# Down-projection of a gated MLP: seven half-size products in place of the plain product

## The chip, the core and the metric

One core of a Trainium2 chip runs the whole layer as one program. The metric is the device time of that program in microseconds (us); the time before, 3258.98 us, is the median of three runs (3258.03 to 3262.15). TensorE multiplies, VectorE and ScalarE work on SBUF and PSUM, GpSimd on SBUF alone, and SyncE's queue (SP) issues nearly all transfers between HBM and SBUF.

## The reference, cut to what matters

The layer has a token-mixing sublayer and a channel-mixing sublayer. Only the second one's end is touched. x is 2048 tokens x 1024, `w_up` 1024 x 5632, `w_down` 2816 x 1024, all float32.

```python
def conv_ffn(x, conv_w, conv_b, w_up, w_down):
    h = x @ w_up
    h = causal_depthwise_conv_width_3(h, conv_w) + conv_b
    gate, val = jnp.split(h, 2, axis=-1)
    return (jax.nn.silu(gate) * val) @ w_down

ffn = conv_ffn(x, ...)
x = layer_norm(ALPHA * x + ffn, ln2_g, ln2_b)      # the output, 2048 x 1024
```

## The kernel before

A float32 product is made of three passes: each operand is split into a high part (rounded to the multiplier's format, ScalarE) and a low part (the rest, VectorE), and `mm3` adds high x high, high x low and low x high into one PSUM bank. `split` and `split_new` make the parts.

The stages follow each other: projections, attention, `mix_out`, `ffn_up`, `ffn_down`. Each is a generator, and `run_to_end` calls `turn` after each step; `store` puts a transfer on a list that `turn` issues on SP one step later. Tiles come from pools: `T` is a slot of 4 KB a partition (42 of them), `M` one of 2 KB (8), `PS1` a PSUM bank (4), `PS2` a pair of banks (2 pairs). A new tile waits until the last user of its slot is done. The build orders each engine's instructions by when it reckons that they can start, so an engine's order is near the order of the program text but not the same.

`ffn_up` takes the tokens in two halves of 1024 (`hf`) and in each half the 22 column blocks (`NF`) of gate and value, already as seven half-size products (`product`, k = 0 to 6); in the second half the blocks run backwards and their split weights come back from HBM (`slot_back`, one block ahead). `after` adds the products from PSUM, `conv` does the convolution, the gate and the store of the block `h[hf][f]` (128 features x 1024 tokens) to HBM, spread over the next block's seven steps. After the last block the rest of `conv` runs by itself (line 1759).

`ffn_down` runs over `seq`: five parts of row blocks (4, 4, 4, 2 and 2 blocks of 128 tokens) x 22 feature blocks f. Each step loads one weight block of 128 x 1024 and the part's columns of one h block three steps ahead (`load`), splits them one step ahead (`split`), and issues 3 matmuls for each row block and column half: 24 a step in parts of four. The sums of a part stay in all 8 banks, or in 4. In the last step of a part VectorE adds ALPHA times the residual row (`load_rows`) to each bank, and `norm_stages` does the layer norm of each row block in stages, one a step: "A" takes the sums on ScalarE, "D" on VectorE; with "-" the gain and shift are VectorE's, otherwise the letters name the engines ("P" is GpSimd). The last two row blocks of all take "D".

Of the kernel before, what the change touches and what calls it, by code (L numbers as in the profile page):

```python
# [18 lines left out]
S, D = 2048, 1024  # L19
# [224 lines left out]

class Kern:
# [156 lines left out]
    def setup(self):  # L402
# [25 lines left out]
        self.d_h = [[self.DT([P, 2 * G], name="h") for _ in range(NF)] for _ in range(2)]  # L428
        self.I = {}
# [1210 lines left out]
    def ffn_up(self):  # L1640
# [6 lines left out]
        nc, cw = self.nc, self.cw  # L1647
        hl = self.C([P, 2 * NF, 2], name="hl")
# [43 lines left out]
        prep = Share(self.operands(1), 40, 7 * (NF - 2))  # L1692
        for i in range(2 * NF):
# [30 lines left out]
            for k in range(7):  # L1724
                ps = self.product(i, k)
                if i == NF - 1:
                    self.xo[k] = None
                    self.ffn_operand(1, k)
                if k:
                    after(k - 1, done)  # L1730
# [15 lines left out]
                if hf == 0 and f:  # L1746
                    prep.tick()
                    if i == NF - 2 and k == 6:
                        prep.flush()
                yield 2.7  # L1750
# [8 lines left out]
        for _ in work:  # L1759
            yield  # L1760

    def ffn_down(self):

        nc = self.nc
        parts = [(0, 4), (4, 4), (8, 4), (12, 2), (14, 2)]
        seq = [(n, f) for n in range(len(parts)) for f in range(NF)]
        raw, ready, rows = {}, {}, {}

        def load(j):
            if j >= len(seq):  # L1770
                return
            n, f = seq[j]
            b, m = parts[n]
            w, h = self.T([P, D]), self.M([P, m * P])
            nc.sync.dma_start(w, self.a["w_ffn_down"][0, f * P:(f + 1) * P, :])
            nc.sync.dma_start(h, self.d_h[b // 8][f][:, (b % 8) * P:(b % 8 + m) * P])
            raw[j] = w, h

        def split(j):
            if j >= len(seq):  # L1780
                return
            w, h = raw.pop(j)
            hp = self.T([P, 2, h.shape[1]], F32R)
            self.split(hp[:, 0], hp[:, 1], h)
            ready[j] = self.split_new(w), hp

        def load_rows(n):
            b, m = parts[n]
            rows[n] = []
            for i in range(b, b + m):  # L1790
                t = self.T([P, D])
                nc.sync.dma_start(t, self.d_x1[i // 8][i % 8])  # L1792
                rows[n].append(t)

        for j in range(3):
            load(j)
        split(0)
        gb = self.load_norm("ln2_g", "ln2_b")
        norming = []

        def norm_tick():
            for gen in list(norming):
                if next(gen, "end") == "end":
                    norming.remove(gen)

        for j, (n, f) in enumerate(seq):
            b, m = parts[n]
            if f == 0:
                if m == 4:
                    t = [self.PS2(), self.PS2()]  # L1810
                    banks = [t[i][:, c * 512:(c + 1) * 512] for i in range(2) for c in range(2)]
                    banks += [self.PS1() for _ in range(4)]
                elif n % 2:
                    banks = [self.PS1() for _ in range(4)]
                else:
                    t = [self.PS2(), self.PS2()]
                    banks = [t[i][:, c * 512:(c + 1) * 512] for i in range(2) for c in range(2)]
                load_rows(n)
            load(j + 3)
            split(j + 1)  # L1820
            (wh, wl), hp = ready.pop(j)
            for i in range(m):
                r = slice(i * P, (i + 1) * P)
                for c in range(2):
                    cs = slice(c * 512, (c + 1) * 512)
# [99 lines left out]
```

## Time and profile before

| | |
|---|---|
| time, median of 3 runs | 3258.98 us |
| profiled execution | 3255.52 us |
| its span, first to last instruction | 3253.7 us |
| TensorE busy | 3106.2 us, 95% |
| VectorE busy | 2415.8 us, 74% |
| ScalarE busy | 1613.8 us, 50% |
| GpSimd busy | 642.8 us, 20% |
| mean granted clock of TensorE | 0.984 of full speed |

Busy time is the sum of an engine's instruction durations over the span. The granted clock is the share of full speed that the chip gave TensorE. In the profile PE is TensorE, PEld its weight loads, DVE VectorE, ACT ScalarE, POOL GpSimd, SPq the transfer queue; tiles are named by pool: b is a `T` tile, m an `M` tile, p PSUM, xtmp and xraw scratch tiles. Line 133 is the helper through which all instructions are recorded, so rows are told apart by tiles and shapes.

### The profile page before, as it was taken

The numbers are of one execution on the slowest core, as the hardware profiler recorded it, in microseconds if no ns is written. First come the engines' busy times: TensorE is split into PE (matmuls) and PEld (weight loads), VectorE is DVE, ScalarE is ACT, GpSimd is POOL, SyncE is SP. The second block draws the span as 40 slices with busy tenths as digits, with TensorE's granted clock in tenths as the row PEclk, the third lists the DMA queues.
The fourth block names the chain that finished last, engine by engine and source line by source line (L and its number), as shares of the span: only waits on it lengthen the run. The fifth ranks groups of instructions, "written<-read, shape, count | busy, mean of one in ns | idle before, by whom it ended". The sixth has DMA issues, their size and how long they took to land. (4 is left out here: it accounts for less than half of the span.)

```text
span 3253.7 us, 44390 instructions
## 1 busy us (share of the span) xinstructions
PE 3106.2 (95%) x15014; PEld 2585.8 (79%) x15014; DVE 2415.8 (74%) x4642; ACT 1613.8 (50%) x3068; POOL 642.8 (20%) x592
## 2 busy tenths in 40 slices
PE   8998899999999999699999999999999999999998
PEld 8886688888888787488787877878788887888876
DVE  5589987987799989988766799889855555453465
ACT  3365746874678777577411244444432232442343
POOL 2027410010010211000412244445111111000000
PEclk9999899999999999899999999999999999999999
DMA  7667784754575332211546788788666665653554
GB/s 250 233 203 275 247 329 160 259 213 166 177 265 205 118 105 62 93 59 62 200 143 208 262 281 297 285 298 295 245 213 217 225 228 199 234 197 109 205 222 154
DMA packets 306833, 666.88 MB, mean 205 GB/s; under 512 B 25322, under 2 KB 130222, under 8 KB 306606
## 3 DMA queue, kind: packets, MB, share of 16 engines
q1 hardware_dynamic: 297966, 648.31, 56.6%
q10 hardware_dynamic: 8640, 15.73, 1.3%
q8 instruction: 119, 1.95, 0.2%
q14 instruction: 108, 0.88, 0.1%
HBM read 434.67 MB, written 229.28 MB: 204 GB/s over the span
## 5 line engine op out<-in xcount | busy, mean ns | idle before, releaser
L133 PE MATMUL p<-b,b 128*128 128x512 f32 (+3 forms) x12832 | 2888.3, 381 | 104.6 <-ACT b L133 37.9
L133 PEld LDWEIGHTS p<-b,b 128*128 128x128 f32 x12832 | 2305.6, 190 | 559.4 <-ACT b L133 40.7
L133 ACT ACTIVATE b<-p 128x512 fp32r<-128x512 f32 (+11 forms) x618 | 351.5, 603 | 245.8 <-PE p L133 235.5
L133 DVE TENSOR_TENSOR b<-p,b 128x512 fp32r<-128x512 f32 (+5 forms) x574 | 362.7, 652 | 148.5 <-PE p L133 102.7
L133 ACT ACTIVATE b<-b 128x1024 fp32r<-128x1024 f32 (+2 forms) x310 | 265.8, 874 | 305.3 <-DVE b L133 94.0
L133 ACT ACTIVATE m<-b,F 128x448 bf16<-128x448 f32 (+3 forms) x448 | 366.3, 821 | 87.9 <-DVE F L133 69.3
L133 DVE TENSOR_SCALAR_CACHE_REDUCE m<-b,F 128x512 bf16<-128x512 f32 (+6 forms) x476 | 370.0, 808 | 0.9
L133 DVE TENSOR_TENSOR b<-b,b 128x1024 fp32r<-128x1024 f32 (+4 forms) x224 | 282.9, 1268 | 72.4 <-ACT b L133 48.3
L133 POOL TENSOR_TENSOR b<-b,b 128x1024 f32<-128x1024 f32 (+3 forms) x94 | 231.5, 2464 | 480.5 <-DVE b L133 399.0
L133 DVE SCALAR_TENSOR_TENSOR b<-b,cw,b 128x1022 f32<-128x1022 f32 (+1 forms) x176 | 248.0, 1419 | 94.4 <-ACT b L133 93.5
L133 ACT ACTIVATE b<-m 128x512 fp32r<-128x512 f32 (+1 forms) x248 | 143.9, 587 | 301.0 <-DVE m L133 121.4
L133 ACT ACTIVATE b<-b,cw 128x1024 f32<-128x1024 f32 x88 | 106.8, 1236 | 290.0 <-DVE b L133 290.0
L133 DVE TENSOR_TENSOR b<-m,b 128x512 fp32r<-128x512 f32 (+1 forms) x248 | 163.7, 667 | 86.2 <-ACT b L133 86.0
L133 ACT ACTIVATE b<-b,mx 128x1024 f32<-128x1024 f32 (+2 forms) x192 | 171.7, 896 | 73.9 <-DVE mx L133 71.9
L133 PE MATMUL p<-ident,b 128*128 128x128 f32 x1248 | 194.9, 275 | 9.5 <-DVE b L133 7.3
L133 DVE SCALAR_TENSOR_TENSOR b<-b,ws,b 128x768 f32<-128x768 f32 (+5 forms) x154 | 155.8, 1040 | 49.2 <-ACT b L133 46.6
L133 DVE CUSTOM_DVE_ANT_0 b<-p,b 128x1024 f32<-128x1024 f32 (+2 forms) x192 | 173.5, 906 | 20.5 <-PE p L133 19.7
L133 PEld LDWEIGHTS p<-ident,b 128*128 128x128 f32 x1248 | 152.6, 141 | 43.2 <-DVE b L133 5.5
L133 PE MATMUL p<-kst,b 128*128 128x384 f32 (+3 forms) x656 | 151.0, 361 | 4.8 <-DVE b L133 2.5
L133 DVE SCALAR_TENSOR_TENSOR b<-b,p 128x512 f32<-128x512 f32 x64 | 42.8, 683 | 151.7 <-PE p L133 145.2
L133 ACT ACTIVATE m<-p 128x512 f32<-128x512 f32 (+2 forms) x172 | 100.7, 586 | 74.9 <-PE p L133 69.2
L133 PEld LDWEIGHTS p<-kst,b 128*128 128x128 f32 x656 | 112.8, 191 | 26.3 <-ACT b L133 13.7
(122 smaller groups left out, 1593.0 us busy)
## 6 DMA issues: line engine op xcount, KB each, us to landing
b<-wk SPq DMA_DIRECT2D x339, 512.0 KB
wk<-b SPq DMA_DIRECT2D x211, 512.0 KB
b<-in_w_ffn_down_dram SPq DMA_DIRECT2D x110, 512.0 KB
b<-in_w_ffn_up_dram SPq DMA_DIRECT2D x44, 512.0 KB
h<-b SPq DMA_DIRECT2D x44, 512.0 KB
b<-vv SPq DMA_DIRECT2D x80, 256.0 KB
m<-h SPq DMA_DIRECT2D x66, 256.0 KB
xT<-b SPq DMA_DIRECT2D x32, 512.0 KB
```

The costliest lines, as they stand in the source:

```text
L133: return f(*args, **kw)
```

## The change

`ffn_down` no longer computes rows x weights directly. The 2048 x 2816 matrix h is cut into four quarters (token half x feature half), and so is `w_down` (feature half x column half). Seven products of quarter-size sums (1024 tokens x 1408 features by 1408 x 512) and additions of their results replace the eight quarter products. The order of the products is 0, 4, 3, 5, 2, 6, 1 (`seq` in `Down`), and each runs over its 11 feature blocks (chunks) with the sums of all 8 row blocks in the 8 PSUM banks; the last one, 1, is cut into row blocks 0 to 3, 4 to 5 and 6 to 7.

- The sums of weights are made in the second half of `ffn_up` by `down_sums`, four subtractions on GpSimd for each of 11 blocks, stored to HBM (`d_wt`).
- The sums of h are made in `ffn_down` by `Down.sum`, one operation of 128 x 1024 on GpSimd for each chunk of products 4, 3, 5 and 6; two of them are stored for a later product (`d_hs`).
- `after` in `ffn_down` takes each product out of PSUM into `R0` and `R1` (16 `T` tiles): ScalarE copies products 0 and 4, VectorE adds the others, GpSimd makes two sums.
- Residual rows are loaded and added during products 2 and 6. The norms are queued: row blocks 8 to 15 after product 2 (kind "AP": sums and scaling on ScalarE, gain on GpSimd, shift on VectorE), the others in product 1 ("A-", the last two "D-").
- The first three chunks are loaded, and the first one is split, in the last block of `ffn_up`; the rest of the last `conv` is taken a step at a time in `ffn_down`.

```diff
+class Down:
+    def __init__(self, k):
+        self.k, self.half = k, NF // 2
+        self.seq = [(p, c, 0, 8) for p in (0, 4, 3, 5, 2, 6) for c in range(self.half)]
+        self.seq += [(1, c, a, b) for a, b in ((0, 4), (4, 6), (6, 8)) for c in range(self.half)]
+        self.raw, self.ready, self.kept = {}, {}, {}
+    def sources(self, p, c):
...
+        tokens = {0: (h(0, 0),), 4: (h(1, 0), h(1, 1)), 3: (k.d_hs[0][c], h(0, 0)), 5: (h(0, 0), h(1, 0)),
+                  2: (h(1, 1),), 6: (h(0, 1), k.d_hs[1][c]), 1: (h(0, 1),)}[p]
+        if p in (0, 1, 6):
+            f = c + half * (p > 0)
+            weights = w[f * P:(f + 1) * P, 512 * (p == 6):512 * (p == 6) + 512]
+        else:
+            weights = k.d_wt[{4: 0, 3: 1, 5: 2, 2: 3}[p]][c]
+    def load(self, j):
...
+        for d in tokens:
+            t = self.k.T([P, (b - a) * P])
+            nc.sync.dma_start(t, d[:, a * P:b * P])
+            x.append(t)
+        if a == 0:
+            w = self.k.M([P, 512])
+            nc.sync.dma_start(w, weights)
+    def sum(self, j):
...
+        if len(x) == 2:
+            self.k.nc.gpsimd.tensor_tensor(x[0], x[0], x[1], op=OP.add if p == 4 else OP.subtract)
+            x.pop()
+        if p in (3, 4):
+            self.k.store(self.k.d_hs[0 if p == 4 else 1][c], x[0])
+    def split(self, j):
...
+        if a == 0:
+            v = self.k.T([P, 2, 512], F32R)
+            self.k.split(v[:, 0], v[:, 1], w)
+            if p == 1:
+                self.kept[c] = v
+        else:
+            v = self.kept[c]
+        self.ready[j] = v, self.k.split_new(x)
@@ ffn_up @@
+        sums = Share(self.down_sums(), 8 * (NF // 2), 7 * (NF - 3))
+                if i == 2 * NF - 1:
+                    self.xo[k] = None
+                    if 2 <= k < 5:
+                        down.load(k - 2)
+                    if k == 6:
+                        down.split(0)
+                if i > NF:
+                    sums.tick()
-        for _ in work:
-            yield
+        self.hdone = work
+    def down_sums(self):
...
+        for c in range(half):
+            top = self.extra.tile([P, D], F32, tag="xraw", name=self._name("xraw"))
+            nc.sync.dma_start(top, w[c * P:(c + 1) * P])
+            b21, b22 = tmp(), tmp()
+            nc.sync.dma_start(b21, w[r, :512])
+            nc.sync.dma_start(b22, w[r, 512:])
+            t1, t2 = tmp(), tmp()
+            sub(t1, b12, b11)
+            sub(t2, b22, t1)
+            sub(b22, b22, b12)
+            nc.sync.dma_start(self.d_wt[0][c], t1)
+            sub(b21, b21, t2)
+            nc.sync.dma_start(self.d_wt[1][c], t2)
+            nc.sync.dma_start(self.d_wt[2][c], b22)
+            nc.sync.dma_start(self.d_wt[3][c], b21)
@@ ffn_down @@
+        def norm_tick(start):
             for gen in list(norming):
                 if next(gen, "end") == "end":
                     norming.remove(gen)
+            if queue and start:
+                norming.append(queue.pop(0))
+        def residual(b, y):
+            nc.vector.scalar_tensor_tensor(y, xs.pop(b), ALPHA, y, op0=OP.mult, op1=OP.add)
+        def after(k, i, ps):
+            add = nc.vector.tensor_tensor
+            if k == 0:
+                R0[i] = self.T([P, D])
+                nc.scalar.activation(R0[i][:, lo], ps, AF.Copy)
+            elif k == 4:
+                R1[i] = self.T([P, D])
+                nc.scalar.activation(R1[i][:, lo], ps, AF.Copy)
+                nc.gpsimd.tensor_tensor(R0[i][:, hi], R0[i][:, lo], R1[i][:, lo], op=OP.add)
+            elif k == 3:
+                add(R0[i][:, hi], ps, R0[i][:, hi], op=OP.add)
+            elif k == 5:
+                add(R1[i][:, hi], ps, R0[i][:, hi], op=OP.add)
+                nc.gpsimd.tensor_tensor(R1[i][:, lo], R1[i][:, hi], R1[i][:, lo], op=OP.subtract)
+            elif k == 2:
+                add(R1[i][:, lo], ps, R1[i][:, lo], op=OP.add)
+                queue.append(norm(8 + i, R1[i], "AP"))
+            elif k == 6:
+                add(R0[i][:, hi], ps, R0[i][:, hi], op=OP.add)
+            else:
+                add(R0[i][:, lo], ps, R0[i][:, lo], op=OP.add)
+                queue.append(norm(i, R0[i], "D-" if i >= 6 else "A-"))
+        for j, (k, c, b0, b1) in enumerate(down.seq):
...
+            down.load(j + 3)
+            down.sum(j + 2)
+            down.split(j + 1)
+            if k == 2 and c == 0:
+                gb = self.load_norm("ln2_g", "ln2_b")
+            if k in (2, 6):
+                half = 8 if k == 2 else 0
+                if 1 <= c < 9:
+                    load_residual(half + c - 1)
+                if c >= 3:
+                    residual(half + c - 3, (R1 if half else R0)[c - 3])
+            w, (xh, xl) = down.get(j)
+            for i in range(b0, b1):
+                r = slice((i - b0) * P, (i - b0 + 1) * P)
+                self.mm3(banks[i], xh[:, r], xl[:, r], w[:, 0], w[:, 1], c == 0, c == down.half - 1)
+                if c == down.half - 1:
+                    after(k, i, banks.pop(i))
+            next(self.hdone, None)
+            norm_tick(k == 1 and (b0 or c % 2 == 0) or c % 2 == 1)
             yield
+        while norming or queue:
+            norm_tick(True)
```

## Rows read from the trace of the kernel before

**Rows 1.** The page: busy time of each engine; GB/s moved in 40 equal slices

```profile
PE 3106.2 (95%) x15014; PEld 2585.8 (79%) x15014; DVE 2415.8 (74%) x4642; ACT 1613.8 (50%) x3068; POOL 642.8 (20%) x592
GB/s 250 233 203 275 247 329 160 259 213 166 177 265 205 118 105 62 93 59 62 200 143 208 262 281 297 285 298 295 245 213 217 225 228 199 234 197 109 205 222 154
```

**Rows 2.** Stretch: length; busy PE, PEld, DVE, ACT, POOL; granted clock, DMA share, GB/s

```profile
2360.00:2737.30 377.30, 377.30 (x1665) 312.11 (x1663) 202.53 (x239) 109.01 (x197) 47.93 (x20) 1.00 0.62 219
2737.30:2768.20 30.90, 20.87 (x75) 15.92 (x74) 12.70 (x14) 12.43 (x19) 7.84 (x1) 0.83 0.53 202
2768.20:3110.00 341.80, 341.80 (x1498) 281.94 (x1499) 152.06 (x205) 117.31 (x161) 8.21 (x8) 1.00 0.49 175
2900.00:3000.00 100.00, 100.00 (x442) 82.53 (x441) 38.09 (x54) 33.55 (x48) 2.34 (x3) 1.00 0.45 158
3110.00:3128.00 18.00, 12.29 (x55) 9.84 (x53) 15.63 (x36) 12.95 (x23) 4.11 (x4) 0.90 0.36 121
3128.00:3242.00 114.00, 112.96 (x488) 92.28 (x488) 73.36 (x104) 55.41 (x83) 2.04 (x2) 0.99 0.65 239
3242.00:3253.70 11.70, 0.00 (x0) 0.00 (x0) 8.20 (x20) 0.00 (x0) 1.10 (x2) 0.58 0.22 90
```

**Rows 3.** Timeline of TensorE: start, length, what, count, idle before and releaser

```profile
2714.72 22.60 PE L133 MATMUL p<-b,b 128*128 128x512 f32 x99
2743.64 2.92 PE L133 MATMUL p<-b,b 128*128 128x512 f32 x6 [6.32 <-ACT b L133]
2747.70 17.38 PE L133 MATMUL p<-b,b 128*128 128x512 f32 x66 [1.14 <-DVE b L133]
2768.16 354.06 PE L133 MATMUL p<-b,b 128*128 128x512 f32 x1551 [0.76 <-DVE b L133]
3127.92 61.18 PE L133 MATMUL p<-b,b 128*128 128x512 f32 x262 [5.71 <-DVE b L133]
```

**Rows 4.** Groups by shape in the down-projection: busy, mean ns, idle before

```profile
L133 DVE TENSOR_TENSOR b<-b,b 128x1024 fp32r<-128x1024 f32 x104 | 127.0, 1222 | 42.5 <-ACT b L133 23.6 <-issue 8.5 <-PE p L133 7.8
L133 DVE TENSOR_TENSOR b<-m,b 128x512 fp32r<-128x512 f32 x60 | 41.2, 686 | 56.8 <-ACT b L133 56.8
L133 DVE TENSOR_TENSOR b<-m,b 128x256 fp32r<-128x256 f32 x44 | 18.4, 418 | 7.0 <-ACT b L133 7.0
L133 DVE SCALAR_TENSOR_TENSOR b<-b,nr,b 128x1024 f32<-128x1024 f32 x16 | 20.4, 1277 | 0.1
L133 DVE SCALAR_TENSOR_TENSOR nt<-nr,nv 128x1 f32<-128x1 f32 x16 | 3.4, 210 | 1.5 <-POOL nr L133 1.5
L133 ACT ACTIVATE b<-b 128x1024 fp32r<-128x1024 f32 x103 | 108.1, 1050 | 49.5 <-DMA b<-in_w_ffn_down_dram 40.6 <-PE p L133 7.5 <-DVE b L133 1.1
L133 ACT ACTIVATE b<-m 128x512 fp32r<-128x512 f32 x59 | 36.9, 625 | 82.0 <-PE p L133 74.3 <-DMA m<-h 7.0 <-DVE b L133 0.8
```

**Rows 5.** Groups by shape in the second half of the up-projection

```profile
L133 POOL TENSOR_TENSOR b<-b,b 128x1024 f32<-128x1024 f32 x22 | 52.7, 2397 | 366.7 <-DVE b L133 349.5 <-issue 17.2
L133 DVE TENSOR_TENSOR b<-p,b 128x512 f32<-128x512 f32 x109 | 72.8, 686 | 101.4 <-PE p L133 101.3
```

**Rows 6.** Timelines of VectorE and GpSimd in the up-projection's first half

```profile
2000.54 1.78 DVE L133 TENSOR_TENSOR b<-b,b 128x512 fp32r<-128x512 f32 x1
2007.47 0.68 DVE L133 TENSOR_TENSOR b<-b,b 128x512 fp32r<-128x512 f32 x1
1999.85 1.93 POOL L133 TENSOR_TENSOR m<-m,b 128x512 f32<-128x512 f32 x1 [1.75 <-DMA b<-in_w_ffn_up_dram]
2015.74 1.29 POOL L133 TENSOR_TENSOR m<-b 128x512 f32<-128x512 f32 x1 [2.42 <-DMA b<-in_w_ffn_up_dram]
```

**Rows 7.** Timeline of VectorE at the end of the third part

```profile
3109.98 3.88 DVE L133 SCALAR_TENSOR_TENSOR b<-b,p 128x512 f32<-128x512 f32 x6 [0.38 <-PE p L133]
```

**Rows 8.** GB/s in 40 equal slices of the down-projection, 2768 to 3242

```profile
GB/s 406 399 258 90 141 170 66 0 10 187 344 406 274 223 103 202 73 0 1 160 319 410 329 172 109 139 51 1 0 93 320 395 395 318 11 198 374 378 5 0
```

**Rows 9.** Timeline of VectorE at the end of the kernel

```profile
3239.37 1.37 DVE L133 SCALAR_TENSOR_TENSOR b<-b,p 128x512 f32<-128x512 f32 x2 [17.09 <-PE p L133]
```

More of the change, by code (lines that the diff above doesn't have):

```diff
@@ L428, in setup @@
         self.d_h = [[self.DT([P, 2 * G], name="h") for _ in range(NF)] for _ in range(2)]
+        self.d_wt = [[self.DT([P, 512], name="wt") for _ in range(NF // 2)] for _ in range(4)]
+        self.d_hs = [[self.DT([P, 2 * G], name="hs") for _ in range(NF // 2)] for _ in range(2)]
         self.I = {}
@@ L1647, in ffn_up @@
         nc, cw = self.nc, self.cw
+        down = self.down = Down(self)
         hl = self.C([P, 2 * NF, 2], name="hl")
@@ L1749, in ffn_up @@
                         prep.flush()
+                if i > NF:
+                    sums.tick()
+                    if i == 2 * NF - 2 and k == 6:
+                        sums.flush()
                 yield 2.7
@@ L1760, in ffn_up @@
             yield
     def ffn_down(self):
[L1764 to L1801, printed above, removed]
+        nc, down = self.nc, self.down
+        R0, R1 = [None] * 8, [None] * 8
+        lo, hi = slice(0, 512), slice(512, 1024)
+        queue, norming, gb, xs = [], [], None, {}
+        def norm(b, y, kind):
+            def gen():
+                act = kind[0] == "A"
+                gain, shift = (nc.gpsimd, nc.vector) if kind[1] == "P" else (None, None)
+                yield from self.norm_stages(y, gb, act, gain, shift, self.out[0, b * P:(b + 1) * P, :])
+            return gen()
@@ L1810, in ffn_down @@
+        for j, (k, c, b0, b1) in enumerate(down.seq):
+            if c == 0:
+                banks = {}
+                if k != 1:
                     t = [self.PS2(), self.PS2()]
[L1811 to L1814, printed above, removed]
-                else:
-                    t = [self.PS2(), self.PS2()]
-                    banks = [t[i][:, c * 512:(c + 1) * 512] for i in range(2) for c in range(2)]
@@ L1818, in ffn_down @@
[L1818 to L1825, printed above, removed]
-                    ps = banks[2 * i + c]
-                    self.mm3(ps, hp[:, 0, r], hp[:, 1, r], wh[:, cs], wl[:, cs], f == 0, f == NF - 1)
-                    if f == NF - 1:
-                        y = rows[n][i]
-                        nc.vector.scalar_tensor_tensor(y[:, cs], y[:, cs], ALPHA, ps, op0=OP.mult, op1=OP.add)
-                if f == NF - 1:
-                    kind = "D--" if b + i >= NB - 2 else SWITCH
-                    act, gain, shift = kind[0] == "A", None, None
-                    norming.append(self.norm_stages(y, gb, act, gain, shift,
-                                                    self.out[0, (b + i) * P:(b + i + 1) * P, :]))
@@ L1836, in ffn_down @@
-            if f == NF - 1:
-                del rows[n]
-                banks = ps = t = y = None
-            norm_tick()
+                    banks = dict(enumerate([x[:, h] for x in t for h in (lo, hi)] + [self.PS1() for _ in range(4)]))
+                elif b0 == 0:
+                    banks = {i: self.PS1() for i in range(4)}
+                else:
+                    t = self.PS2()
+                    banks = {b0: t[:, lo], b0 + 1: t[:, hi]}
+                t = None
+            down.load(j + 3)
```

47 lines of the change are left out of this document (41 added, 6 removed).

## The prediction, made before the change was run

> **What bounds the kernel now.** I read the page first: TensorE is busy for 95% of the span [rows 1]. Then the busy time by stretches [rows 2]: the up-projection runs to 2737.3 us, the down-projection from there to 3242, and what is left behind it is 11.7 us without a matmul. In the middle of the down-projection, 2900 to 3000, TensorE is busy for 100.00 of 100 us at the full granted clock (level 2.4 GHz) and starts 442 matmuls, one each 0.226 us. VectorE (152 of 342 us) and ScalarE (117) stand well behind it there [rows 2]. So what the stage costs is the number of its matmuls times 0.226 us, plus what is lost between.
>
> The count is fixed by the code: 16 row blocks x 22 contraction blocks x 2 column halves x 3 passes = 2112 matmuls, 477.3 us. The stage takes 2737.3 to 3241.8 = 504.5 us, so 27.2 us are lost. The timeline of TensorE [rows 3] says where. At the change of stages it stands still for 6.3, 1.1 and smaller pieces; the 6+66 matmuls done by 2768 need 16.3 us at full pace and took 30.9, at a mean clock of 0.83 [rows 2]: 14.6 lost. From 2768.2 to 3110 it does 1512 matmuls without a gap. From 3110 to 3241.8 the last 528 need 119.3 us and take 131.8: 12.5 lost, of them 5.7 idle where VectorE was at the norms of four rows [rows 3], the rest mostly the clock, 0.90 around it [rows 2].
>
> **Matmuls.** Seven products of 8 row blocks x 11 contraction blocks x 3 passes = 1848, with the same shapes (128x128 stationary, 512 columns moving) and the same order within a group of three. 264 fewer x 0.226 = **-59.7 us**, all on the path.
>
> **Change of stages.** Today, by the code, all loads but the first three stand on SP's queue behind the last block's store, which waits for GpSimd, and the convolution's last work stands before the first splits on ScalarE and VectorE; TensorE's 6.3 us wait is for ScalarE [rows 3]. Afterwards the first three chunks (a chunk: one contraction block of a product) are loaded during products 2 to 4 of the last up-projection block and the first is split in its product 6, about 11 us later, and the convolution's remainder is spread behind the first chunks. The first product reads blocks of h stored long before; the last block's store, now on SP behind several chunks' loads, is needed only by the second product, 60 us on. The norm's vectors are loaded in the fifth product instead of here. PSUM is free: two double tiles are not used by the up-projection, the four single ones are needed last. Between 0 and 14.6 us remain; I take 1, since nothing late stands before the first chunk: **-13.6 us**.
>
> **Weight sums in the up-projection.** 44 GpSimd operations of 128x512, half of 2.40 us each [rows 5] = 53 us, where GpSimd is busy 48 of 377 us; 23 MB of loads and stores in about 360 us, 64 GB/s on top of 219 [rows 2], 283 in all, where slices of the page with a full TensorE hold 297 and 298 [rows 1]. The sums stand on SP between the loads of the next block's weights, which are issued a whole block (19 us) before use. GpSimd's product after the gate stands behind at most one sum; its store waits that much. VectorE's evictions read PSUM and go on at 0.686 [rows 5]. Cost: 0, covered by the one-block lead; without it some us a block x 20 blocks. I take 0, bound 0 to 3.
>
> **Work per chunk.** A chunk is 24 matmuls, 5.42 us. ScalarE splits 1.05 + 0.62 = 1.7 us, VectorE 1.22 + 0.69 = 1.9 [rows 4]. Four products (44 chunks) add one GpSimd sum of 2.40 [rows 5]. The last chunk of a product adds 8 evictions of 0.69 [rows 5], one behind each row's last matmul, as today; the next product's first bank is free after the first two. After two products GpSimd has 8 additions of 1.2 more, needed a product (60 us) later. New waits: GpSimd for two loads, ScalarE's split for GpSimd, and two products' stores of sums, which wait on SP for GpSimd with the next loads behind them. Each is covered as long as several chunks are ready ahead. That they can be shows in the transfer slices: in the middle of a part the rate falls to 0 and 1 GB/s [rows 8], every buffer is full. Afterwards 8, then 16 of the 42 large buffers hold results, two the norm's vectors and up to three residual rows; 21 remain, at five a chunk four chunks, 22 us. Cost 0.
>
> **Transfers.** The products with a stored sum move 1.84 MB a chunk, 339 GB/s; the sixth product (two operands, weights, a residual row, some outputs) 19.7 MB in 59.7 us, 330 on average and about 390 for eight chunks. Today's bursts reach 399 to 410 [rows 8]. Cost 0, bound 21 us (rival below).
>
> **Norms.** The real crowding is at the end. Row blocks 8 to 15 are normed over the sixth product and the start of the seventh, row blocks 0 to 5 within the seventh. The seventh is 264 matmuls, 59.7 us, with chunks of only 2.7 and then 1.36 us. VectorE there: splits 11 x 1.38 + 22 x 0.42 = 24.4; five shifts of 1.22 = 6.1 and the five rows' small operations 4.5; six norms of 2 x 1.28 + 0.8 = 20.4 [rows 4]; eight evictions 5.5: 61 us. So it is full, without slack. Today's nearest place is the end of the third part: four norms and the evictions at once, TensorE ran on with ready chunks from 3110 to 3122.2, then stood for 5.7 [rows 3, 7], 12.5 lost with what follows. Bounds: 0 (the lead absorbs all) to 28 (rival). I take **12**, so no change against today's 12.5.
>
> **End.** After the last matmul two rows are normed on VectorE as today; today four evictions stand there [rows 9], then two, but the second row's norm enters one step later. 0, give or take 2.
>
> **Sum.** 3255.5 (profiled execution, its span 3253.7 and 1.8 around it) - 59.7 - 13.6 - 0.5 = 3181.7. The profiled execution lay 3.5 under the median of the runs, 3258.98; so **3185 us**.
>
> **Rivals.**
> (1) GpSimd and VectorE take turns. Where a GpSimd addition and a VectorE subtraction from two SBUF inputs meet, VectorE's goes from 0.68 to 1.78 and GpSimd's from 1.29 to 1.93 [rows 6]: together they take about the sum of both. In the sixth product: VectorE 11 x 1.9 + 8 residual rows x 1.28 + 3 x 1.22 = 35, GpSimd 14 x 2.40 = 34: 69 against 59.7, +9. In the seventh 61 + 5 x 2.40 = 73, +13. With two drops of the clock at 3 us each, +28 on a stage without losses (3173.5): **3201**. For it: the row; against: evictions from PSUM and the small operations don't meet GpSimd, and the lead takes up some. 22%.
> The Trainium skill has a rule for it (SBUF — State Buffer, "Who interferes with whom"): a VectorE instruction with two SBUF inputs and a GpSimd instruction that reads SBUF exclude each other for the whole instruction. By that rule the time would be this rival's; the rows show both stretched, rather than one unhindered and one waiting, which comes to the same sum.
> (2) Transfers hold only some 300 GB/s when loads and stores mix, as in the slices of the up-projection's first half, 281 to 298 [rows 1]: 0.7 us more for each of 22 chunks and 6 in the sixth product, +21: **3206**. Against: 318 to 410 in today's bursts [rows 8]. 10%.
> (3) All is absorbed, the end too: **3172**. 9%.
> (4) The other side: the lead is lost in the products with a sum. If only one chunk is under way, load (1.3 MB at 400 GB/s, 3.3), GpSimd 2.4, ScalarE 1.05 and VectorE 1.2 stand in a row before 5.4 us of matmuls, 8 us x 44 chunks = +350: **about 3530**. It decides from 1.7 us a chunk, where the 73 us gained are gone; that needs fewer than about two chunks ready, through an order of waits on SP (store of a sum before the next loads) that holds back loads. Against it the 21 free buffers. 4%, and about half as much for a mild form that ends near the time before.
> That the change does not bring fewer matmuls is excluded by the loops.
>
> **How the numbers follow.** Forecast 3185, 53% with its own range 3174 to 3196; (1) 22%, (2) 10%, (3) 9%, (4) 6% with its mild form. The range takes in (1) and (2) and stops short of (3)'s far side: 3168 to 3212. About 0.2% (6.5 us) is what a measurement can tell from no change: faster 0.94, same 0.02, slower 0.04.
>
> **What would show it.** Right: 1848 matmuls of the stage at 0.226; no gap over 2 us at 2737; granted clock 1.0 through the first five products; gaps only in the last 100 us, ended by VectorE. Rival 1: VectorE's 128x1024 subtractions well over 1.22 on average, gaps in the sixth product. Rival 2: ScalarE or GpSimd waiting for transfers in products with a sum. Wrong: a gap at each chunk, ended by GpSimd or a load; a longer up-projection.

## The result, and the profile of the changed kernel

The changed kernel took 3225.71 us (median of four runs, 3220.54 to 3227.69), the kernel before in the same comparison 3260.57 (four runs, 3258.03 to 3262.35): a ratio of 0.9903, with a 95% interval of 0.9891 to 0.9915. That is 35 us faster; 74 were forecast, and the time lies 14 us above the range. The profiled execution took 3227.53 us, 45.8 more than the forecast's sum for it (3181.7).

First the page, against [rows 1]: busy time of each engine, and GB/s in 40 equal slices of the span.

```profile
PE 3053.4 (95%) x14750; PEld 2542.7 (79%) x14750; DVE 2474.6 (77%) x4622; ACT 1595.9 (49%) x3048; POOL 876.1 (27%) x704
GB/s 251 236 183 279 252 319 150 264 220 200 129 261 256 116 103 66 67 96 53 144 202 173 239 277 287 297 297 294 306 271 290 284 221 216 279 259 339 257 214 90
```

TensorE gave up 264 matmuls and 52.8 us of busy time, but its share of the span is again 95%: time without a matmul has not shrunk, it has moved. Where to, the windows tell, against [rows 2] (stretch: length; busy time of TensorE, its weight loads, VectorE, ScalarE, GpSimd; granted clock, share of the transfer engines, GB/s). The up-projection of the second token half now ends at 2765.2, the down-projection at 3214.4.

```profile
2348.80:2527.50 178.70, 168.96 (x732) 138.13 (x733) 85.74 (x104) 49.72 (x88) 62.09 (x41) 0.99 0.80 287
2527.50:2765.20 237.70, 237.69 (x1049) 196.87 (x1050) 136.11 (x160) 71.64 (x127) 31.40 (x13) 1.00 0.67 241
2800.00:2860.00 60.00, 60.00 (x266) 49.26 (x265) 36.06 (x21) 21.53 (x31) 34.87 (x13) 1.00 0.99 368
3062.00:3121.70 59.70, 59.67 (x262) 49.11 (x262) 48.04 (x70) 33.59 (x50) 29.50 (x16) 1.00 0.70 234
3121.70:3143.20 21.50, 0.04 (x1) 0.04 (x1) 17.42 (x29) 11.75 (x19) 9.03 (x6) 0.55 0.49 167
3143.20:3160.00 16.80, 16.80 (x64) 13.71 (x65) 9.96 (x16) 4.47 (x8) 0.00 (x0) 0.86 0.23 69
3214.40:3225.70 11.30, 0.00 (x0) 0.00 (x0) 7.49 (x19) 0.00 (x0) 1.09 (x2) 0.58 0.23 93
```

The first row is inside the up-projection, which was to be left as it was: 10 of 179 us have no matmul, where the kernel before had a matmul running in every one of 377 us [rows 2]. The fifth is a hole of 21.5 us behind the sixth product. Between them everything is full, the change of stages at 2765.2 included.

TensorE's timeline shows the same as single gaps, against [rows 3] (start, length, count; in brackets the idle time before and what ended it).

```profile
2325.74 20.71 PE L133 MATMUL p<-b,b 128*128 128x512 f32 x84 [3.05 <-DVE b L133]
2348.84 110.67 PE L133 MATMUL p<-b,b 128*128 128x512 f32 x480 [2.39 <-DVE b L133]
2461.26 19.33 PE L133 MATMUL p<-b,b 128*128 128x512 f32 x84 [1.75 <-ACT m L133]
2482.54 19.35 PE L133 MATMUL p<-b,b 128*128 128x512 f32 x84 [1.94 <-DMA b<-wk]
...
2527.51 534.05 PE L133 MATMUL p<-b,b 128*128 128x512 f32 x2351 [2.52 <-ACT b L133]
3062.01 59.67 PE L133 MATMUL p<-b,b 128*128 128x512 f32 x262 [0.44 <-DVE b L133]
3143.16 51.23 PE L133 MATMUL p<-b,b 128*128 128x512 f32 x215 [21.48 <-DVE b L133]
3196.79 8.50 PE L133 MATMUL p<-b,b 128*128 128x512 f32 x36 [2.40 <-DVE b L133]
```

So the difference to the forecast can be measured between three marks that every kernel here has: the first matmul behind the last transpose of x for the second token half (2236.5 before, 2244.3 after), ScalarE's first convolution step of the last up-projection block (2738.1 before, 2765.2 after), and the end of the last matmul. The stretch between the first two is called "up" below, that between the last two "down"; differences are taken before rounding. Down without any loss is 1848 x 0.226 = 417.6 us.

| | before | forecast | after | missed by |
|---|---|---|---|---|
| to the first mark | 2236.5 | the same | 2244.3 | 7.8 |
| up | 501.6 | 501.6 | 520.9 | 19.4 |
| down | 503.7 | about 430 | 449.2 | 19 |

The first line is no effect of the change: up to 2259 us every engine has the same instructions in the same order in all kernels here, and the mark fell between 2232 and 2244 in their profiles: these 7.8 us are scatter. The two others are effects of the change, and they have different causes.

### The first cause: a ring in the up-projection

Here is one turn of it in the changed kernel: SP's queue with the store of h (L1758) and the load of weights for the sums (L1860), GpSimd, and ScalarE. The last two lines are ScalarE's convolution steps of the kernel before.

```profile
2455.62 0.32 SPq L1758 DMA_DIRECT2D h<-b  x1
2461.11 0.55 SPq L1860 DMA_DIRECT2D xraw<-in_w_ffn_down_dram  x1
2476.84 0.32 SPq L1758 DMA_DIRECT2D h<-b  x1
2498.46 0.32 SPq L1758 DMA_DIRECT2D h<-b  x1
...
2469.19 1.30 POOL L133 TENSOR_TENSOR xtmp<-xraw 128x512 f32<-128x512 f32 x1 [13.60 <-DMA xraw<-in_w_ffn_down_dram]
2473.17 1.29 POOL L133 TENSOR_TENSOR xtmp<-xtmp,xtmp 128x512 f32<-128x512 f32 x1
2474.42 2.39 POOL L133 TENSOR_TENSOR b<-b,b 128x1024 f32<-128x1024 f32 x1
...
2476.85 1.24 ACT L133 ACTIVATE b<-b,cw 128x1024 f32<-128x1024 f32 x1 [12.61 <-POOL b L133]
2481.80 0.57 ACT L133 ACTIVATE m<-p 128x512 f32<-128x512 f32 x1
...
2700.06 2.38 ACT L133 ACTIVATE b<-b,cw 128x1024 f32<-128x1024 f32 x2 [12.32 <-DVE b L133]
2719.10 2.38 ACT L133 ACTIVATE b<-b,cw 128x1024 f32<-128x1024 f32 x2 [12.32 <-DVE b L133]
```

SP's store of h waits for GpSimd's gate product. The load for the next weight sums stands behind that store and eight other transfers on SP and is issued 5.49 us later; its data are there 8.08 us after that; the four subtractions take 5.23; the next gate product stands behind them on GpSimd, and its end releases the next store, 2.42 later. Together 21.22 us from store to store, and 21.62 in the next turn. A block of the up-projection needs 19.04 (2700.06 to 2719.10 in the kernel before). Each turn pushes the block: ScalarE's convolution step waits for GpSimd, the eviction `m<-p` (a finished sum taken out of PSUM) stands behind it, and TensorE, at 2482.54 and before, waits for a bank or for weights that SP also issues late. ScalarE's idle 12.61 us by themselves are no loss: the kernel before has 12.32 there, ended by VectorE. What is new is that GpSimd ends them, at the pace of the ring. The list of waits from 2360 to 2530 (engine and tile, for what: us in total, times, longest) says it in two lines:

```profile
POOL xtmp L133 <- DMA xraw<-in_w_ffn_down_dram: 97.9, 7, 15.5
ACT b L133 <- POOL b L133: 79.5, 6, 14.6
```

### The second cause: VectorE behind GpSimd in the sixth product

The sixth product's last matmul ends at 3121.68. Its eight sums wait in all eight banks for VectorE, which comes to them at 3142.43. What stands before them is in VectorE's timeline; GpSimd's follows.

```profile
3085.09 2.48 DVE L133 TENSOR_TENSOR b<-m,b 128x512 fp32r<-128x512 f32 x1 [0.76 <-ACT b L133]
3090.34 2.35 DVE L133 SCALAR_TENSOR_TENSOR nt<-nr,nv 128x1 f32<-128x1 f32 x1 [0.44 <-POOL nr L133]
3114.87 1.23 DVE L133 TENSOR_TENSOR b<-b,b 128x1024 f32<-128x1024 f32 x1 [2.55 <-POOL b L133]
3120.12 2.32 DVE L133 TENSOR_TENSOR nr<-nr,nt 128x1 f32<-128x1 f32 x1
3128.10 1.83 DVE L133 TENSOR_TENSOR b<-b,b 128x1024 f32<-128x1024 f32 x2 [2.45 <-POOL b L133]
3133.34 2.35 DVE L133 TENSOR_TENSOR nmr<-nm,nr 128x1 f32<-128x1 f32 x1
3142.43 1.87 DVE L133 TENSOR_TENSOR b<-p,b 128x512 f32<-128x512 f32 x3
...
3084.61 2.41 POOL L133 TENSOR_TENSOR b<-b,b 128x1024 f32<-128x1024 f32 x1 [2.25 <-ACT b L133]
3090.28 2.39 POOL L133 TENSOR_TENSOR b<-b,b 128x1024 f32<-128x1024 f32 x1
3120.04 2.38 POOL L133 TENSOR_TENSOR b<-b,b 128x1024 f32<-128x1024 f32 x1 [0.40 <-ACT b L133]
3133.33 2.34 POOL L133 TENSOR_TENSOR b<-b,b 128x1024 f32<-128x1024 f32 x1 [0.66 <-ACT b L133]
```

VectorE is not even busy all the time: 48.0 of the product's 59.7 us. It waits for GpSimd in two ways. In the open: the shift of a norm (`b<-b,b` 128x1024) waits 2.55 and 2.45 us for GpSimd's gain. And hidden as busy time: an operation on one number per partition, 0.21 us in [rows 4], is recorded with 2.32 to 2.35 when it starts just behind a GpSimd operation of 2.34 to 2.39; the split that started 0.48 us behind a GpSimd operation ends 0.55 behind that one's end. In these rows GpSimd started first and keeps its length, 2.34 to 2.41.

The Trainium skill states this (SBUF — State Buffer, "Who interferes with whom"): two SBUF inputs on VectorE and a read of SBUF by GpSimd shut each other out for the whole instruction. These rows agree, more plainly than [rows 6] did: the one that comes second waits in full.

By an estimate these waits are of the size of the hole. From 3062 to 3143 VectorE did 14 splits of 128x512 at 1210 ns instead of 686, eight shifts at 1766 instead of 1230, and three small operations some 2.15 us too long: 7 + 4 + 6 us hidden, and 5 in the open, 22 to 23 us.

Over the whole stage the groups by shape answer to [rows 4]: mean ns and idle time by group, 2740 to the end.

```profile
L133 DVE TENSOR_TENSOR b<-b,b 128x1024 fp32r<-128x1024 f32 x66 | 103.7, 1571 | 21.9 <-ACT b L133 17.4 <-PE p L133 3.9 <-issue 0.6
L133 DVE TENSOR_TENSOR b<-m,b 128x512 fp32r<-128x512 f32 x77 | 100.8, 1309 | 62.1 <-ACT b L133 62.1
L133 DVE TENSOR_TENSOR b<-p,b 128x512 f32<-128x512 f32 x46 | 29.9, 685 | 21.1 <-PE p L133 21.1
L133 DVE TENSOR_TENSOR b<-b,b 128x1024 f32<-128x1024 f32 x8 | 14.1, 1766 | 5.0 <-POOL b L133 5.0
L133 POOL TENSOR_TENSOR b<-b,b 128x1024 f32<-128x1024 f32 x54 | 154.0, 2857 | 146.1 <-DMA b<-h 59.0 <-DVE b L133 34.4 <-PE p L133 22.1
```

The splits grew from 1222 to 1571 and from 686 to 1309 ns, 23 + 48 = 71 us in the stage; the eviction, which reads PSUM and one SBUF tile, has stayed at 685. GpSimd's mean over the stage is 2857 ns, above the 2.4 us of the rows above: it has its share of the waits. Most of the 71 us is covered by the lead of ready chunks. In the sixth product it is not.

### The profile page after: what moved, and what is told of

The parts are those of the page before. It is cut to its first block, busy times and chain, and to the rows that moved or that the text cites. A ratio compares the mean times of both kernels' runs of the same rounds, so it can differ in the third digit from the quotient of the medians.

```text
span 3225.7 us, 44051 instructions
## 1 busy us (share of the span) xinstructions
PE 3053.4 (95%) x14750; PEld 2542.7 (79%) x14750; DVE 2474.6 (77%) x4622; ACT 1595.9 (49%) x3048; POOL 876.1 (27%) x704
## 5 line engine op out<-in xcount | busy, mean ns | idle before, releaser
L133 PE MATMUL p<-b,b 128*128 128x512 f32 (+3 forms) x12568 | 2834.4, 382 | 126.4 <-DVE b L133 53.5
L133 PEld LDWEIGHTS p<-b,b 128*128 128x128 f32 x12568 | 2260.8, 190 | 572.1 <-DVE b L133 55.8
L133 POOL TENSOR_TENSOR b<-b,b 128x1024 f32<-128x1024 f32 (+4 forms) x154 | 386.8, 2516 | 454.3 <-DVE b L133 254.5
L133 DVE TENSOR_TENSOR b<-p,b 128x512 f32<-128x512 f32 (+3 forms) x614 | 388.1, 654 | 139.1 <-PE p L133 93.2
L133 ACT ACTIVATE b<-b 128x512 fp32r<-128x512 f32 (+3 forms) x299 | 236.0, 807 | 343.9 <-DVE b L133 118.8
L133 DVE SCALAR_TENSOR_TENSOR b<-b,cw,b 128x1023 f32<-128x1023 f32 (+1 forms) x176 | 249.2, 1425 | 136.1 <-ACT b L133 135.3
L133 DVE TENSOR_TENSOR b<-b,b 128x1024 fp32r<-128x1024 f32 (+6 forms) x221 | 283.5, 1292 | 56.5 <-ACT b L133 39.3
L133 ACT ACTIVATE b<-m 128x512 fp32r<-128x512 f32 x215 | 133.0, 627 | 285.2 <-DVE m L133 125.0
L133 DVE TENSOR_TENSOR b<-m,b 128x512 fp32r<-128x512 f32 x215 | 203.1, 953 | 83.9 <-ACT b L133 83.7
L133 POOL TENSOR_SCALAR b<-b 128x1024 fp32r<-128x1024 f32 (+2 forms) x50 | 53.3, 1069 | 350.3 <-DMA b<-in_w_in_dram 175.2
```

Of the source, the lines that this page charges most:

```text
L133: return f(*args, **kw)
```

## The experiments

Each kernel is the changed one with one to four edits. Up, down and the gap in front of the seventh product are read from its profile between the marks above; ratios are against the kernel before on the same chip, with 95% intervals.

| kernel | time, us | ratio | up | down | gap |
|---|---|---|---|---|---|
| before | | 1 | 501.6 | 503.7 | |
| after | 3225.71 | 0.9903 [0.9891, 0.9915] | 520.9 | 449.2 | 21.48 |
| e1 weight sums without subtractions | 3202.11 | 0.9828 [0.9812, 0.9845] | 501.7 | 448.9 | 21.36 |
| e2 loads for them a block ahead | 3209.19 | 0.9853 [0.9839, 0.9868] | 509.4 | 448.5 | 21.38 |
| e3 norms without GpSimd's gain | 3206.99 | 0.9844 [0.9829, 0.9858] | 523.4 | 435.8 | 5.16 |
| e4 no sums in product 6 | 3211.73 | 0.9862 [0.9847, 0.9876] | 520.8 | 441.7 | 13.86 |
| e5 e2 + e3, sums a block later | 3198.38 | 0.9819 [0.9799, 0.9839] | 513.8 | 435.2 | 4.66 |
| e6 gain on VectorE | 3211.05 | 0.9858 [0.9833, 0.9883] | 523.6 | 439.1 | 10.78 |
| e7 early start undone | 3231.63 | 0.9915 [0.9890, 0.9939] | 523.8 | 459.1 | 21.38 |
| e8 e5 + e4 | 3194.24 | 0.9804 [0.9785, 0.9824] | 517.7 | 426.0 | 1.11 |
| e9 gate product on VectorE + e3 | 3193.47 | 0.9805 [0.9791, 0.9818] | 507.8 | 434.3 | 6.89 |
| e10 e9 + residuals earlier | 3198.09 | 0.9815 [0.9801, 0.9828] | 510.3 | 436.6 | 3.04 |
| e11 e9, sums a block later | 3195.80 | 0.9814 [0.9801, 0.9828] | 509.2 | 433.7 | 7.36 |
| e12 e11 + e4 | 3183.26 | 0.9779 [0.9766, 0.9792] | 507.6 | 426.4 | 1.67 |

### Up-projection: ring or transfers

**e1.** The same bytes are loaded and stored, at nearly the same places of SP's queue, but GpSimd makes no weight sums: the raw quarters are stored in their place, so four of the products get other weights.

```diff
-            t1, t2 = tmp(), tmp()
-            sub(t1, b12, b11)
+            t1, t2 = b11, b12
             yield
-            sub(t2, b22, t1)
             yield
-            sub(b22, b22, b12)
...
-            sub(b21, b21, t2)
```

> The four GpSimd subtractions of each weight block are left out of the up-projection; the same bytes are loaded and stored (raw quarters in place of the sums), so products 4, 3, 5 and 2 multiply the wrong weights. Theory A (a ring of waits: GpSimd stands at its first subtraction for a load that SP issued late, the gate product stands behind it on GpSimd, the store of h behind that on SP, the next load behind that): with no subtraction GpSimd never waits for these loads, the stage of 22 blocks runs at 19.0 us a block again and ends about 19 us earlier; total about 3206. Theory B (the 64 GB/s of extra transfers make the split weights come late): nothing changes, 21.5 us a block around 2400 to 2530, total about 3225.

```profile
2340.94 419.39 PE L133 MATMUL p<-b,b 128*128 128x512 f32 x1849 [1.17 <-DVE b L133]
```

Up fell to 501.7, the length before the change, and down stayed. From 2360 to 2700 this kernel moves 267 GB/s with TensorE busy for 340.00 of 340 us, where the kernel before moves 219: the added traffic cost nothing. All 19 us hang on the subtractions on GpSimd, not on the transfers.

**e2.** All four quarters are loaded one block before they are used, so that no subtraction waits for a load that stands behind the store of h. `fetch` issues the four loads of a block into tiles of their own.

```diff
...
+        nxt = fetch(0)
         for c in range(half):
+            b11, b12, b21, b22 = nxt
+            nxt = fetch(c + 1) if c + 1 < half else None
...
```

> The four quarters of a weight block are loaded one block ahead into other buffers, so that GpSimd finds them there; the subtractions, the stores and the bytes stay. Theory A (ring of waits through one late load): blocks of 19.0 us, the up-projection ends about 19 us earlier, total about 3206. Theory B (transfers): unchanged, about 3225. Theory C (VectorE and GpSimd take turns at SBUF and so the evictions and the convolution are late): about half stays, 3215.

The gaps inside the blocks went, and up came down to 509.4. What stayed is one long gap where the token halves change; behind it TensorE runs for 255 us without one:

```profile
2341.49 255.07 PE L133 MATMUL p<-b,b 128*128 128x512 f32 x1116 [7.92 <-DVE b L133]
2597.12 163.22 PE L133 MATMUL p<-b,b 128*128 128x512 f32 x719 [0.56 <-DMA b<-wk]
```

There VectorE has the splits of the new half's operands, and seven subtractions of GpSimd fell among them. The meeting of the two engines is thus in the up-projection too, at a place where TensorE waits for VectorE in the kernel before already (1.13 us in front of 2334.48).

### The hole behind the sixth product

**e3.** The norms of row blocks 8 to 15 take kind "A-": gain and shift are VectorE's. One operation of 128x1 for each row block stays on GpSimd, as in all kinds.

```diff
-                queue.append(norm(8 + i, R1[i], "AP"))
+                queue.append(norm(8 + i, R1[i], "A-"))
```

> Row blocks 8 to 15 are normed as kind A- (gain and shift in two VectorE operations) instead of AP (ScalarE scaling, GpSimd gain, VectorE shift). Theory D (the chain VectorE - GpSimd - VectorE - ScalarE - GpSimd - VectorE of these norms, with VectorE's small operations caught behind GpSimd's 2.4 us, makes VectorE late for the evictions of product 6): the 21.5 us gap behind product 6 shrinks below 5, total about 3203. Theory E (VectorE simply has too much work there, and A- gives it 1.3 us more for each row): the gap stays or grows, 3225 to 3235. Theory F (the chunk sums of product 6 on GpSimd are what stretches VectorE): the gap shrinks by less than half, about 3217.

```profile
3121.62 50.48 PE L133 MATMUL p<-b,b 128*128 128x512 f32 x215 [5.16 <-DVE b L133]
```

The hole shrank from 21.48 to 5.16 us, with a new one of 2.89 before the sixth product, and down from 449.2 to 435.8, although VectorE has eight operations of 128x1024 more to do. GpSimd's help cost 13 us.

**e4.** The operand sums of the sixth product are not made: it multiplies its first operand alone, and so part of the output is not computed.

```diff
+        if p == 6:
+            x.pop()
         if len(x) == 2:
```

> Product 6 leaves out its eleven operand sums on GpSimd and multiplies its first operand alone; both operands are still loaded. Theory D (the norms' chain through GpSimd): the gap behind product 6 shrinks only by what the chain waited behind sums, to 12 to 18 us, total about 3218. Theory F (the chunk sums): the gap goes below 5 us, total about 3203. Theory E (too much work on VectorE alone): the gap stays near 20.

```profile
3125.10 52.14 PE L133 MATMUL p<-b,b 128*128 128x512 f32 x216 [13.86 <-DVE b L133]
```

The hole shrank to 13.86, down to 441.7. So both users of GpSimd in that product have a part in it: 13.4 us go with the gains, 7.5 with the sums.

**e6.** The gains move to VectorE, but the norm keeps its stages, one a step, as with GpSimd. It tells what GpSimd's part costs from what the number of stages costs.

```diff
-                gain, shift = (nc.gpsimd, nc.vector) if kind[1] == "P" else (None, None)
+                gain, shift = (nc.vector, nc.vector) if kind[1] == "P" else (None, None)
```

> The gain of the norms of row blocks 8 to 15 is moved from GpSimd to VectorE; the scaling stays on ScalarE, so the stages of the norm stay five. VectorE gets 8 x 1.2 us more, GpSimd 8 x 2.4 us less. Theory D1 (GpSimd's gain itself: it blocks VectorE's port and stands in the chain): the gap behind product 6 falls from 21.5 to about 5, as with kind A-. Theory D2 (the five stages over three engines, each in order, whoever does the gain): the gap stays above 12. Theory E (too much work on VectorE): the gap grows beyond 21.5.

A gap of 10.78 and 439.1 for down, between the two. Of the 13.4 us of e3, 10.1 come from the gain no longer being GpSimd's, 3.3 from the fewer stages.

**e5** joins e2 and e3 and lets the weight sums begin one block later.

```diff
-        sums = Share(self.down_sums(), 8 * (NF // 2), 7 * (NF - 3))
+        sums = Share(self.down_sums(), 8 * (NF // 2), 7 * (NF - 4))
...
-                if i > NF:
+                if i > NF + 1:
                     sums.tick()
```

> Three edits together: the loads of the weight sums one block ahead, their start one block later (away from the splits at the change of token halves, where one gap of 7.9 us was left), and row blocks 8 to 15 normed as A-. If the two losses are independent: the up-projection takes what it took before (502 us from the last transposes of the token sums to its end, against 522 after), the gap behind product 6 is about 5 us, total about 3187, ratio 0.979. If the wait only moves on (the next thing late is VectorE, for the evictions): about 3197.

Down was as in e3. The gap at the change of token halves went as meant (1.17 is left, before 1.13). Up to there VectorE and ScalarE have the same order of work in e2, e5 and the kernel before, and from the first mark to the block behind the change they need 103.2, 97.0 and 98.0 us: the subtractions among the splits make the difference. But up took 513.8, and the time was 3198 where about 3187 was expected: waits of the ring's kind came back between 2405 and 2627. SP itself waited 49 us there for stores of earlier sums to leave the tiles of the early loads, with the block's other transfers behind it.

```profile
2466.42 97.11 PE L133 MATMUL p<-b,b 128*128 128x512 f32 x420 [3.27 <-ACT m L133]
...
2577.63 38.35 PE L133 MATMUL p<-b,b 128*128 128x512 f32 x168 [1.44 <-DMA b<-wk]
```

Loading early loosens the ring; the gate product still stands behind the subtractions. SP's waits alone do not make these gaps: e2 has 50.6 us of the same waits between 2345 and 2630, and TensorE runs through there but for 0.56 us. What e5 has besides is the later begin; how it brings the gaps is not shown.

**e8** is e5 without the sums of product 6 (the edit of e4).

> As e5_both, and product 6 leaves out its eleven operand sums on GpSimd (its first operand alone is multiplied). If the rest of the gap behind product 6 (5 us and 3 ahead of it) comes from VectorE's splits meeting GpSimd's sums: both go to under 1 us and the time is 8 to 12 us under e5_both. If it comes from VectorE's own work (residual rows, norms, evictions): within 3 us of e5_both.

The hole is closed (1.11) and down is 426.0, with 8.4 lost of a stage of 417.6. What was left of it in e5 (4.66) was splits that met GpSimd's sums.

**e9.** The ring is cut at another link: the gate product of the second token half is VectorE's, so neither the store of h nor ScalarE waits for GpSimd. The loads stay where the change has them. The norms are those of e3.

```diff
-            nc.gpsimd.tensor_tensor(a[0], a[0], a[1], op=OP.mult)
+            (nc.vector if i >= NF else nc.gpsimd).tensor_tensor(a[0], a[0], a[1], op=OP.mult)
```

> The weight sums stay as in the changed kernel (their loads late, on one buffer), but the gate product of the second token half goes from GpSimd to VectorE, so nothing of the convolution stands behind a waiting subtraction; and row blocks 8 to 15 are normed as A-. Theory A (ring of waits): with the ring cut here the up-projection takes 502 to 506 us from the last transposes of the token sums to its end, though GpSimd waits for its loads as long as before; gaps behind product 6 as with A- alone, about 5 us; total about 3187, ratio 0.979. If the late loads themselves or the transfers were the cause, the blocks stay near 21 us and the total is near 3206.

Up is 507.8, and from 2340 on it has no gap:

```profile
2340.26 420.04 PE L133 MATMUL p<-b,b 128*128 128x512 f32 x1852 [0.85 <-DVE b L133]
```

The waits of 2360 to 2530 show that the ring was cut and not the late loads: GpSimd still waits 80.4 us for them, ScalarE no longer for GpSimd.

```profile
ACT b L133 <- DVE b L133: 120.6, 18, 12.4
POOL xtmp L133 <- DMA xraw<-in_w_ffn_down_dram: 80.4, 7, 12.9
```

The 6.3 us that remain over 501.6 lie at the change of token halves: from the first mark to the block that starts at 2340 it takes 104.3 us, in the changed kernel 104.6, in the kernel before 98.0, in e1 without subtractions 98.1. So the 19.4 us of the changed kernel are about 6 there and 13 in the ring. At 3193.5 us this kernel beats the changed one by 32 us and the one before by 65.

**e10** moves the residual rows 0 to 7 from the sixth product into the fifth, to relieve VectorE in the sixth.

```diff
-            if k in (2, 6):
-                half = 8 if k == 2 else 0
...
+            if k == 2:
+                for half in (8, 0):
```

> As e9_gate_on_vector, and the residual rows of row blocks 0 to 7 are loaded and added in product 2, which has no operand sums, instead of product 6. That takes 8 x 1.3 to 1.5 us of VectorE and 4 MB of loads out of product 6. If VectorE's load where GpSimd's sums run decides the rest of the gaps around product 6 (2.7 and 4.7 us): both under 1.5 us, total 5 to 9 us under e9_gate_on_vector, about 3180, ratio 0.977. If not: the same time within 3 us; if the rows crowd product 2 instead: a gap of some us behind product 2.

Missed: the gap before the seventh product fell from 6.89 to 3.04, but one of 4.87 came before the sixth. The wait moved with the work.

**e11** is e9 with sums that begin a block later, against the 6.3 us at the change of halves.

> The gate product of the second token half on VectorE, the norms of row blocks 8 to 15 without GpSimd, and the weight sums begun one block later, so that they no longer meet VectorE's work at the change of token halves. Ring theory: the remaining gaps of the run before this one lay in the first block behind the change of halves, where splits of VectorE met GpSimd's subtractions; without that meeting the up-projection takes 502 to 503.5 us (507.9 with the sums begun one block earlier), and no gap over 1 us stands in it. The down-projection stays at 434 to 436. Time 3186 to 3190, ratio 0.978 to 0.979. Rival: the meeting is not the cause but the first sums themselves (their loads late on SP), which then only move one block on: up-projection 506 to 510, time unchanged at about 3193.

It tested nothing. The build orders instructions by when it reckons that they can start, and put the first subtraction where it had been: 33.7 us behind the first mark, in e9 33.8. Every engine has the same instructions in the same order in both traces, so the two are one kernel, and the intervals of their ratios, 0.9805 and 0.9814, overlap. So that the meeting makes these 6.3 us rests on e1 and on e5, where the first subtraction did move (to 2349.8) and the gap went. A rival falls with e1: in the changed kernel and in e9 the build also puts some splits of this stretch later than in the kernel before, but e1 has the changed kernel's order there but for one split, and needs 98.1 us.

**e12** is e11 without the sums of product 6, so like e4 it does not compute all of the output; these are the 11 sums of its chunks (44 of that shape on GpSimd in e9, 33 here), not 13.

> As the kernel beside it, and the operand sums of the sixth product (13 of the GpSimd operations of the down-projection, the tokens' sum of product 6) are left out, so that part of the output is not computed. If the two causes found, the ring in the up-projection and the meeting of GpSimd's sums with VectorE's splits in the sixth product, are all that the forecast missed, the time falls to the forecast's sum: up-projection 502 to 504, down-projection 425 to 427, time 3177 to 3184, ratio 0.975 to 0.977. If a third cause is left, it stays over 3188.

Down 426.4 as expected; up 507.6, a miss, for the reason of e11. The time, 3183.26, is where the forecast was, but by another sum: 6 us more in up, about 3.5 less in down. With ring, gains and the sixth product's sums out of the way no single gap over 2.1 us is left at the end of down, as TensorE's timeline shows:

```profile
3100.77 49.27 PE L133 MATMUL p<-b,b 128*128 128x512 f32 x216 [1.67 <-DVE b L133]
3152.13 15.81 PE L133 MATMUL p<-b,b 128*128 128x512 f32 x61 [2.10 <-DVE b L133]
```

### The change of stages

**e7.** The first loads, the first split and the rest of the convolution go back to the start of the down-projection.

```diff
-                    if 2 <= k < 5:
-                        down.load(k - 2)
-                    if k == 6:
-                        down.split(0)
...
-        self.hdone = work
+        for _ in work:
+            yield
+        self.hdone = iter(())
...
+        for j in range(3):
+            down.load(j)
+        down.split(0)
```

> The first three chunks are loaded and the first is split at the start of the down-projection instead of in the last block of the up-projection, and the rest of the convolution is done in one piece ahead, as in the kernel before. If the early start is worth what the loss at the change of stages showed: a gap or gaps of about 10 us at the change, the clock lower for some 30 us behind it, 10 to 15 us longer in all, total about 3238. If the order of the build would have moved the first loads forward anyway: under 3 us, about 3227.

The gap of 6.32 us for ScalarE is back, of the same length as in [rows 3], and the clock behind it falls (0.90 from 2765 to 2800, where the changed kernel has 1.00). Down is 9.9 us longer. By the time alone the two kernels are not told apart (the intervals overlap): the profile of e7 reached the first mark some 7 us earlier.

```profile
2766.68 2.50 PE L133 MATMUL p<-b,b 128*128 128x512 f32 x5 [6.32 <-ACT b L133]
2765.00:2800.00 35.00, 32.90 (x134) 26.55 (x135) 25.00 (x27) 19.16 (x26) 12.13 (x2) 0.90 0.60 225
```

## Why the prediction was wrong, step by step

- **Matmuls, -59.7: right.** 15014 - 14750 = 264 fewer, and 266 in 60 us where TensorE is full: 0.226 each.
- **Change of stages, -13.6: right.** There is no gap at 2765, and the clock is 1.00. Undoing it cost 9.9 us in e7, less than the 14.6 that the kernel before loses there; why less is not shown.
- **Transfers, 0: right.** From 2800 to 2860 the chunks with a stored sum moved 368 GB/s beside a TensorE busy for 60.00 of 60 us, and e1 shows the up-projection's added traffic to be free. Rival 2 falls.
- **Weight sums, "covered by the one-block lead", 0 to 3: wrong, 19.4.** Two sentences of this step failed. "GpSimd's product after the gate stands behind at most one sum": it stands behind four subtractions, and behind the load they wait for. And the lead of one block belongs to the loads of the next up-projection weights, not to the step's own load, which stood on SP behind the store that waits for GpSimd. I named the store and the loads on SP each by itself and did not follow the store to the load to the subtractions to the gate product and back to the store. e1 and e9 cut the loop at different links and remove the gaps within blocks both times. So 13 us are the ring. The other 6 us are subtractions meeting VectorE's splits at the change of halves, which I had left out because evictions read PSUM.
- **Work per chunk, 0: right for the first five products.** TensorE ran in one piece from 2527.51, still in the up-projection, to 3061.56, where the sixth product begins, although the splits were 71 us longer over the stage.
- **Norms, 12: wrong size, 31.6 lost in down.** The place (sixth and seventh product) and the engine were right. What failed is the sum of VectorE's work in the sixth product as three shifts and a price without GpSimd, and the evictions "one behind each row's last matmul, as today". From 3062 to the end of the hole VectorE did eight shifts, each behind a gain, and the splits of product 1; the evictions came 20.8 us behind the last matmul, with all banks full. Rival 1 had the mechanism with 28 us in the stage and 22% of the chances; measured, all loss of down over 417.6 is 31.6. I took the middle against it with the argument that small operations don't meet GpSimd: three did, at 2.32 to 2.35 us instead of 0.2. Its row was misread too: the two operations of [rows 6] took 2.47 us from the first start to the last end, not about the 1.97 that they take apart.
- **End, 0: right.** 11.3 us behind the last matmul, before 11.9.

Rival 1 taken whole (3201) and the loss in up, which no rival had ("a longer up-projection" stands among the signs of being wrong), would have given the measured time within 6 us: 3201 + 19.4 = 3220, beside 3225.7.

## What to carry to other kernels

When work is added to an engine with an in-order queue, follow one turn of the waits around every queue it touches, not each wait by itself: here store, load, subtractions and gate product closed a ring of 21.2 us beside a block of 19.0, and the cut that worked was to take the gate product off the engine with the late work. Free time on GpSimd is not free where VectorE reads two SBUF tiles beside it: price each such meeting with the full length of the other engine's instruction, and look for it where VectorE's work stands before evictions. And after moving an edit in the program text, look in the trace whether the instructions moved at all.

## What the runs showed of the hardware

- An operation of VectorE on 128x1 numbers with two inputs in SBUF lasted 2.32 to 2.35 us right behind the start of a GpSimd operation of 2.34 to 2.39, 0.15 to 0.22 otherwise, and the profile counts that wait as busy.
- In the hole of 21.5 us TensorE's granted clock was 0.55, near the lower of its two levels (1.2 and 2.4 GHz), and 0.86 over the 17 us of matmuls behind it. 64 matmuls took 16.8 us there, 14.5 at 0.226 each, so the hole cost 2.3 us more than its length. In e7 it was 0.90 over the 35 us from 2765, which take in the end of the gap of 6.32.
- One core moved 368 GB/s, loads and stores together, for 60 us without a wait of TensorE.
